# Two-layer hybrid encoder: one split for both key blocks, squares on ScalarE, rotation from SBUF, and head 3's decay moved behind head 0's scores

## The chip, the cores and the metric

The kernel runs on one core of a Trainium2 chip. The metric is the device time of one execution in microseconds (us). The core's engines run beside each other, each with a queue of its own that it works off in order: TensorE (PE in the profile, PEld for its loads of weights) multiplies, VectorE (DVE) and ScalarE (ACT) work elementwise, GpSimd (POOL) does little here, and SyncE (SP) issues the DMAs. Results of TensorE land in PSUM, which is eight banks; operands lie in SBUF.

## The reference

A trunk of two layers. Each has four token mixers beside each other (A to D), merged by gates, and a gated MLP with a convolution. Batch 1, 256 tokens and 16 meta tokens ahead of them; all in float32.

```python
for l in range(DEPTH):                                   # 2 layers, T = 16 + 256 tokens, D_MODEL = 1024
    u = _rms_norm(h, norm_mix_pre[l])
    (a_q, a_k, a_v, b_q, b_k, b_v, b_r, b_g, c_qa, c_kva, c_kr,
     d_q, d_k, d_v, gate_logits) = jnp.split(u @ w_in[l], offsets, axis=-1)
    o_a = _diff_attention(...)   # A: 4 heads, two softmax maps, p0 - lam * p1, RMSNorm over 128 values
    o_b = _gla(...)              # B: 4 heads, both directions, chunks of 64: cumsum of log decay, exp, RMSNorm
    o_c = _mla(...)              # C: 4 heads, queries of 128 + 64 rotated, rank 256 / 128
    o_d = _window_gqa(...)       # D: 8 query heads, 2 key heads, band of 128, sink
    branches = jnp.stack([o_a, o_b, o_c, o_d], axis=2)
    gates = jax.nn.sigmoid(gate_logits.reshape(bsz, T, N_BRANCH, D_MODEL))
    merged = jnp.sum(jnp.einsum('btnw,nwd->btnd', branches, w_branch[l]) * gates, axis=2)
    h = h + _rms_norm(merged @ w_out[l], norm_mix_post[l])
    f = _conv_ffn(_rms_norm(h, norm_ffn_pre[l]), ffn_w_up[l], ffn_conv_w[l], ffn_conv_b[l], ffn_w_down[l])
    h = h + _rms_norm(f, norm_ffn_post[l])
return h[:, N_META:]
```

`_mla` rotates the last 64 of each query head and one key of 64: `x1 * cos - x2 * sin`, `x1 * sin + x2 * cos`. A and B end with an RMSNorm over the 128 values of a head, which needs the sum of squares. In `_gla` the decay of a head is the exponential of a running sum inside chunks of 64.

## The kernel before

Activations are held transposed: features on the 128 partitions, the 272 tokens along the free axis (258 in parts of layer 2). All weights stream once from HBM in blocks of 128x1024 (512 KB): SP's queue loads a block to a `raw` buffer (three of them), ACT casts it to the high half `wh`, and VectorE subtracts that from `raw` to give the low half `wl` (L221, five buffers each). Activations are split in the same way (`split`, L310 to L312: ACT's cast gives the high half, VectorE's subtraction the low half), and each product is three matmuls, high by high, high by low and low by high (`mm3`). A `raw` buffer is reloaded when its `wl` is done. SP's queue holds these loads in order, with the bias loads of A and D (`bA`, `bD`, L283) among them.

Each mixer is a Python generator whose steps are cut by `yield`. `interleave(main, n_main, n_fill, fill)` runs a mixer's steps and puts pieces of other work between them: the next projections, gates and branch products (`pj`, `br` in the profile), some 12 matmuls of 126 ns each at a time. The pairs `N_B1`, `N_B2`, `N_A` and so on are the counts of steps and of fillers for each stage:

```python
interleave(comp_b1(db), *N_B1, fill)      # B: gates, running sums, decay, factors
interleave(comp_b2(db), *N_B2, fill)      # B: keys, states, scores, outputs of each head
...
interleave(comp_a(da), *N_A, fill)        # A, beside gates, B's branch and C's projections
```

A scheduler of the framework then sets each engine's queue from this program order, the data dependencies and its own estimate of durations, so a queue's order is not the program's order, and a change in one place can re-deal the queues of all engines for some distance. An engine that waits holds all that stands behind it in its queue.

PSUM is shared by three pools: `mm` (three banks: projections, `pj`, `qu`, `br`), `sc` (two: scores) and `ax` (three: transposes `tpp`, `tpr`, `tpv`, sums `ps_A`, `ps_B`, outputs `poA`, `poB`, `poC`). A tile of a pool waits until the reader of the tile that had the bank before is done.

The places that the change touches:

- `transpose_p` (A, C, D): for each head, four transposes put the probabilities of two query blocks and two key blocks into one bank (`tpp`), and `split` brings each key block's half to `pth` (ACT) and `ptl` (VectorE); `tpr` holds the 16 remaining keys.
- `square_hl` (A, B): the square of a head's output on VectorE (L520), its cast on ACT (L521), the rest on VectorE (L522); `sum_heads` multiplies both by ones (`ps_A`, `ps_B`), and `aq` (L933) is ACT's copy of `ps_A`.
- `rope` (C): four ACT copies of 32 rows (`sw`, L971) swap the halves, VectorE multiplies them by the sine (L972), the source in PSUM by the cosine with the scale (L976), and adds (L977). The key's rotation has scale 1 and runs in place. `sw` is one tile with one buffer.
- `comp_b1`, the first stage of B: for each head the running sums (L761, L763, both scans), their exponentials, and the products with keys and queries (L769, L770); `factors` after heads 1 and 3; after head 2 also `keys(d, 0)`, after head 3 `states(d, 0)`. `comp_b2` then goes through the heads: keys, states, scores, outputs.

Of the kernel before, what the change touches and what calls it, by code (L numbers as in the profile page):

```python
# [15 lines left out]
AF = mybir.ActivationFunctionType  # L16
# [8 lines left out]
T = 272  # L25
# [13 lines left out]
AHEAD = 2  # L39
GROUP = 4  # L40
N_WARM, N_WARM0 = 12, 16
N_B1, N_B2, N_A, N_CU, N_C, N_D = (8, 24), (15, 17), (24, 30), (7, 12), (20, 24), (35, 36)
LAM_INIT = [0.8 - 0.6 * math.exp(-0.3 * l) for l in range(DEPTH)]

O_AQ, O_AK, O_AV = 0, 512, 1024
# [72 lines left out]
def hybrid_kernel(ctx: ExitStack, tc: tile.TileContext, hT0, w, pc_in, p2_in, cc_in, oh_in, tab_in, gl_in, out):  # L118
# [354 lines left out]
    for l in range(DEPTH):  # L473
# [9 lines left out]
        with ExitStack() as scope:  # L483
# [33 lines left out]
            def square_hl(src):  # L517
                sq, sqh, sql = [tmp.tile([P, T], dt, name="sq", tag=f"sq{i}", bufs=1)[:, cs]
                                for i, dt in enumerate((F32, F32R, F32R))]
                V.tensor_mul(sq, src[:, cs], src[:, cs])  # L520
                S.copy(sqh, sq)  # L521
                V.tensor_sub(sql, sq, sqh.bitcast(F32))  # L522
                return sqh, sql
# [106 lines left out]
            def transpose_p(pts, pair):  # L630
                pth, ptl, ptr = pts
                tp = axb("tpp")
                for qt in range(2):
                    for kc in range(2):
                        PE.transpose(tp[:, kc * 256 + qt * 128:kc * 256 + qt * 128 + 128],
                                     pair[qt][:, kc * 128:kc * 128 + 128], ident)
                for kc in range(2):
                    split(pth[:, kc, 16:T].rearrange("p (a b) -> p a b", a=2),
                          ptl[:, kc, 16:T].rearrange("p (a b) -> p a b", a=2),
                          tp[:, kc * 256:kc * 256 + 256].rearrange("p (a b) -> p a b", a=2)[:, :, ::-1])  # L640
                tr = axb("tpr")
                for qt in range(2):
                    PE.transpose(tr[:16, qt * 128:qt * 128 + 128], pair[qt][:, 256:272], ident)
                put_rem(ptr, 16, 256, tr[:16, :256].rearrange("p (a b) -> p a b", a=2)[:, :, ::-1])
# [81 lines left out]
            def comp_b1(d):  # L726
# [29 lines left out]
                    V.tensor_copy(mq[b, hs, 1:2], two[b, hs, 1:2])  # L756

                G.memset(dec[64:128, :, 0:1], 1.0)
                for h in range(4):
                    b_ = x1[h][0:64, :]  # L760
                    V.tensor_tensor_scan(b_, C("smask", 0, 64), b_, 0.0, ALU.mult, ALU.add)  # L761
                    b_ = x1[h][64:128, ::-1]
                    V.tensor_tensor_scan(b_, C("smask", 64, 128)[:, ::-1], b_, 0.0, ALU.mult, ALU.add)  # L763
                    x3 = cf("x3")
                    act(LN_EXP_SET, x3, x1[h], AF.Exp, scale=-1.0 / 16)
                    act(LN_EXP_SET, x2[h], x1[h], AF.Exp, scale=1.0 / 16)
                    S.copy(dec[0:64, h, :], x2[h][0:64, 15::64])
                    S.copy(dec[64:128, h, 1:5], x2[h][64:128, 16:T:64])
                    V.tensor_mul(ks[h], ks[h], x3)  # L769
                    V.tensor_mul(qs[h], qs[h], x2[h])  # L770
                    if h % 2:
                        factors(slice(h - 1, h + 1))
                    if h == 2:
                        keys(d, 0)
                    if h == 3:
                        states(d, 0)
                    yield

            def by_chunk(t):
                return t.rearrange("p (c t) -> p c t", c=4)  # L780
# [31 lines left out]
            def comp_b2(d):  # L812
# [39 lines left out]
                for h in range(4):  # L852
                    if h:
                        states(d, h)
                        yield
                        norm(h - 1)
                    if h < 3:
                        keys(d, h + 1)
                    scores(h)
                    yield  # L860
                    outputs(h)
                    yield
                yield
# [101 lines left out]
            def rope(dst, src, rows, c0=0, scale=1.0):  # L965

                sw = tmp.tile([P, T], F32, name="sw", tag="sw", bufs=1)
                c = slice(c0, T)
                for b_ in range(0, rows, 32):
                    o = b_ ^ 32  # L970
                    S.activation(sw[b_:b_ + 32, c], src[o:o + 32, c], AF.Copy, scale=scale)  # L971
                V.tensor_mul(sw[:rows, c], sw[:rows, c], C("sin", 0, rows)[:, c])  # L972
                if scale == 1.0:
                    V.tensor_mul(dst[:, c], src[:, c], C("cos", 0, rows)[:, c])
                else:
                    V.scalar_tensor_tensor(dst[:, c], src[:, c], scale, C("cos", 0, rows)[:, c], ALU.mult, ALU.mult)  # L976
                V.tensor_add(dst[:, c], dst[:, c], sw[:rows, c])  # L977

            def proj_c(d, kper):
# [30 lines left out]
            def proj_c_up(d):  # L1010
# [16 lines left out]
                for i in (4, 5, 0, 1, 2, 3):  # L1027
                    ps = mmb("qu")
                    for k in range(2):
                        mm3(ps[:, cs], wq[k][0][:, i * P:(i + 1) * P], wq[k][1][:, i * P:(i + 1) * P], lh[1 + k][:, cs],  # L1030
                            ll[1 + k][:, cs], k == 0, k == 1)
                    qf.append(u(f"cq{i}"))
                    if i >= 4:
                        rope(qf[-1], ps, P, ct, C_SCALE)
                    else:
                        S.activation(qf[-1][:, cs], ps[:, cs], AF.Copy, scale=C_SCALE)
                    if i % 2:
                        yield
                qf[:] = qf[2:] + qf[:2]
# [510 lines left out]
```

## Time and profile before

| | |
|---|---|
| median of 3 runs | 1144.18 us (1143.24 to 1145.17) |
| the profiled execution | 1141.39 us, its span 1139.6 us |
| granted TensorE clock | 0.999 of full speed |
| busy: PE, DVE, ACT | 1115.9 us, 925.2 us, 757.2 us |
| instructions: PE, DVE, ACT | 8678, 2049, 1635 |

The span runs from the first to the last instruction of the core; the time of the execution is 1.8 us longer. The busy time of an engine is the sum of its instructions. A view of waits lists, for each engine, how long it sat idle until another engine (or a DMA) released it, by the names of the two operations. In a timeline each row is an instruction with its start, its duration, and in brackets the idle time just ahead of it and what ended that. Layer 1's mixers run from about 40 to 300 us, layer 2's from about 600 to 900.

### The profile page before, as it was taken

The numbers are of one execution on the slowest core, as the hardware profiler recorded it, in microseconds if no ns is written. First come the engines' busy times: TensorE is split into PE (matmuls) and PEld (weight loads), VectorE is DVE, ScalarE is ACT, GpSimd is POOL, SyncE is SP. The second block draws the span as 40 slices with busy tenths as digits, with TensorE's granted clock in tenths as the row PEclk, the third lists the DMA queues.
The fourth block names the chain that finished last, engine by engine and source line by source line (L and its number), as shares of the span: only waits on it lengthen the run. The fifth ranks groups of instructions, "written<-read, shape, count | busy, mean of one in ns | idle before, by whom it ended". The sixth has DMA issues, their size and how long they took to land.

```text
span 1139.6 us, 22838 instructions
## 1 busy us (share of the span) xinstructions
PE 1115.9 (98%) x8678; PEld 1077.4 (95%) x8678; DVE 925.2 (81%) x2049; ACT 757.2 (66%) x1635; POOL 12.9 (1%) x57
## 2 busy tenths in 40 slices
PE   9999999999999999999999999999999999999997
PEld 8999889999999999999999998999999999999986
DVE  7977986898977799995479868968989769999843
ACT  7855776777765767665458557867787657766632
POOL 1000000000000000000000000000000000000000
PEclk9999999999999999999999999999999999999999
DMA  7642454445646356655546534554356462655552
GB/s 265 219 147 98 130 160 148 139 116 135 179 142 215 109 172 202 183 161 175 181 142 219 148 100 134 144 165 155 115 142 171 164 241 98 204 196 193 185 185 74
DMA packets 60914, 183.73 MB, mean 161 GB/s; under 512 B 10443, under 2 KB 17739, under 8 KB 60420
## 3 DMA queue, kind: packets, MB, share of 16 engines
q1 hardware_dynamic: 60148, 181.36, 51.6%
q8 instruction: 68, 1.11, 0.4%
q10 hardware_dynamic: 656, 0.91, 0.2%
q14 instruction: 42, 0.34, 0.1%
HBM read 180.03 MB, written 2.21 MB: 160 GB/s over the span
## 4 chain that ended last, share of the span: by engine, by line
PE 80%; DVE 8%; ACT 7%; DMA 2%; issue 2%; SPq 0%; DVEq 0%; ACTq 0%
PE pj L183 52%; PE dn L183 6%; PE br L183 6%; PE dt L183 5%; DMA raw<-wst 2%; DVE wl L221 2%; ACT wh L221 2%; PE sc L183 1%; PE poD L183 1%; PE poB L183 1%; PE at L183 1%; PE tpp L186 1%; PE scm L183 1%; ACT p L607 1%; PE kvu L183 1%
## 5 line engine op out<-in xcount | busy, mean ns | idle before, releaser
L183 PE MATMUL pj<-xh,wh 128*128 128x272 f32 (+1 forms) x1888 | 546.6, 292 | 7.3 <-ACT xh L350 3.1
L183 PE MATMUL pj<-xl,wh 128*128 128x272 f32 (+1 forms) x1888 | 540.1, 287 | 0.0
L183 PE MATMUL pj<-xh,wl 128*128 128x272 f32 (+1 forms) x1888 | 540.1, 287 | 0.0
L221 DVE TENSOR_TENSOR wl<-raw,wh 128x1024 fp32r<-128x1024 f32 (+2 forms) x322 | 386.6, 1204 | 105.0 <-ACT wh L221 102.5
L221 ACT CAST wh<-raw 128x1024 fp32r<-128x1024 f32 (+2 forms) x322 | 332.7, 1035 | 192.9 <-PE pj L183 85.1
L183 PEld LDWEIGHTS pj<-xh,wh 128*128 128x128 f32 x1888 | 354.7, 189 | 12.9 <-ACT xh L350 3.7
L183 PEld LDWEIGHTS pj<-xl,wh 128*128 128x128 f32 x1888 | 356.1, 189 | 1.4 <-issue 0.4
L183 PEld LDWEIGHTS pj<-xh,wl 128*128 128x128 f32 x1888 | 355.6, 189 | 0.7 <-issue 0.2
L1357 ACT ACTIVATE cv<-u,pc 128x272 f32<-128x272 f32 (+1 forms) x88 | 52.9, 605 | 12.5 <-DVE u L1355 12.1
L183 PE MATMUL dn<-ah,wh 128*128 128x272 f32 x176 | 51.0, 290 | 0.0
L183 PE MATMUL dn<-al,wh 128*128 128x272 f32 x176 | 50.7, 288 | 0.0
L183 PE MATMUL dn<-ah,wl 128*128 128x272 f32 x176 | 50.5, 287 | 0.0
L1361 DVE SCALAR_TENSOR_TENSOR cv<-u,pc,cv 128x271 f32<-128x271 f32 (+1 forms) x88 | 43.0, 489 | 1.8
L607 ACT ACTIVATE p<-p,st 128x272 f32<-128x272 f32 x68 | 35.1, 516 | 13.8 <-DVE st L605 13.8
L1359 DVE SCALAR_TENSOR_TENSOR cv<-u,pc,cv 128x271 f32<-128x271 f32 (+1 forms) x88 | 42.9, 487 | 1.2 <-ACT cv L1357 0.9
L1202 DVE TENSOR_TENSOR gt<-pj,rs_x 128x272 f32<-128x272 f32 (+1 forms) x64 | 27.4, 429 | 14.3 <-PE pj L183 13.8
L1355 DVE TENSOR_TENSOR u<-pj,rs_x 128x272 f32<-128x272 f32 (+1 forms) x88 | 36.9, 425 | 0.0
L183 PE MATMUL dt<-wh,al 128*128 128x512 f32 x88 | 34.8, 395 | 0.0
L183 PE MATMUL dt<-wh,ah 128*128 128x512 f32 x88 | 34.7, 395 | 0.0
L183 PE MATMUL dt<-wl,ah 128*128 128x512 f32 x88 | 34.5, 392 | 0.0
L183 PEld LDWEIGHTS dn<-al,wh 128*128 128x128 f32 x176 | 33.1, 188 | 0.0
L183 PEld LDWEIGHTS dn<-ah,wh 128*128 128x128 f32 x176 | 33.1, 188 | 0.0
(390 smaller groups left out, 1904.7 us busy)
## 6 DMA issues: line engine op xcount, KB each, us to landing
raw<-wst SPq DMA_DIRECT2D x306, 512.0 KB, 3.7
raw<-wst SPq DMA_DIRECT2D x12, 384.0 KB, 3.2
bD<-bvec SPq DMA_DIRECT2D x16, 256.0 KB, 5.2
bA<-bvec SPq DMA_DIRECT2D x8, 400.0 KB, 5.0
hT<-hT SPq DMA_DIRECT2D x1, 1088.0 KB, 6.6
h_dram<-hT SPq DMA_DIRECT2D x1, 1088.0 KB
hT<-h_dram SPq DMA_DIRECT2D x1, 1088.0 KB, 6.2
raw<-wst SPq DMA_DIRECT2D x4, 256.0 KB, 4.5
```

Source lines behind the costliest of these rows:

```text
L183: self.note(nc.tensor.matmul(*args, **kw))
L186: self.note(nc.tensor.transpose(*args, **kw))
L221: pair = S.copy(wh[:, c], raw[:, c]), V.tensor_sub(wl[:, c], raw[:, c], wh[:, c].bitcast(F32))
L607: S.activation(p, p, AF.Exp, scale=-1.0, bias=st[:, 0:1], accum_out=st[:, 1:2])
L1202: V.tensor_mul(f[:, ct:T], (yield from pj(ct))[:, ct:T], RS[:, ct:T])
L1355: V.tensor_mul(u_[:, ct:T], ps[:, ct:T], RS[:, ct:T])
L1357: S.activation(t[:, cd:T], u_[:, cd:T], AF.Identity, scale=PCc("cw1", c), bias=PCc("cb", c))
L1359: V.scalar_tensor_tensor(t[:, lo:T], u_[:, lo - 1:T - 1], PCc("cw0", c), t[:, lo:T], ALU.mult, ALU.add)
L1361: V.scalar_tensor_tensor(t[:, cd:T - 1], u_[:, cd + 1:T], PCc("cw2", c), t[:, cd:T - 1], ALU.mult, ALU.add)
```

## The change

It has four parts. `transpose_p` splits both key blocks in one operation for each engine (512 columns in place of twice 256). `square_hl` takes the square on ACT. `rope` for the queries first copies the PSUM bank to SBUF with the scale on ACT, and VectorE multiplies that copy by the cosine; the bank then has readers on ACT only. In B, the decay of head 3 and the factors of heads 2 and 3 move from the first stage into the second, behind the scores of head 0; `keys(d, 0)` and `states(d, 0)` become steps of their own, and each of the two stages counts one step more, with as many fillers as before.

```diff
@@ -39,7 +39,7 @@
 AHEAD = 2
 GROUP = 4
 N_WARM, N_WARM0 = 12, 16
-N_B1, N_B2, N_A, N_CU, N_C, N_D = (8, 24), (15, 17), (24, 30), (7, 12), (20, 24), (35, 36)
+N_B1, N_B2, N_A, N_CU, N_C, N_D = (9, 24), (16, 17), (24, 30), (7, 12), (20, 24), (35, 36)
 LAM_INIT = [0.8 - 0.6 * math.exp(-0.3 * l) for l in range(DEPTH)]
 
 O_AQ, O_AK, O_AV = 0, 512, 1024
@@ -517,7 +517,7 @@
             def square_hl(src):
                 sq, sqh, sql = [tmp.tile([P, T], dt, name="sq", tag=f"sq{i}", bufs=1)[:, cs]
                                 for i, dt in enumerate((F32, F32R, F32R))]
-                V.tensor_mul(sq, src[:, cs], src[:, cs])
+                S.activation(sq, src[:, cs], AF.Square)
                 S.copy(sqh, sq)
                 V.tensor_sub(sql, sq, sqh.bitcast(F32))
                 return sqh, sql
@@ -634,10 +634,9 @@
                     for kc in range(2):
                         PE.transpose(tp[:, kc * 256 + qt * 128:kc * 256 + qt * 128 + 128],
                                      pair[qt][:, kc * 128:kc * 128 + 128], ident)
-                for kc in range(2):
-                    split(pth[:, kc, 16:T].rearrange("p (a b) -> p a b", a=2),
-                          ptl[:, kc, 16:T].rearrange("p (a b) -> p a b", a=2),
-                          tp[:, kc * 256:kc * 256 + 256].rearrange("p (a b) -> p a b", a=2)[:, :, ::-1])
+                split(pth[:, :, 16:T].rearrange("p k (a b) -> p k a b", a=2),
+                      ptl[:, :, 16:T].rearrange("p k (a b) -> p k a b", a=2),
+                      tp.rearrange("p (k a b) -> p k a b", k=2, a=2)[:, :, :, ::-1])
                 tr = axb("tpr")
                 for qt in range(2):
                     PE.transpose(tr[:16, qt * 128:qt * 128 + 128], pair[qt][:, 256:272], ident)
@@ -756,7 +755,9 @@
                     V.tensor_copy(mq[b, hs, 1:2], two[b, hs, 1:2])
 
                 G.memset(dec[64:128, :, 0:1], 1.0)
-                for h in range(4):
+
+                def decay(h):
+
                     b_ = x1[h][0:64, :]
                     V.tensor_tensor_scan(b_, C("smask", 0, 64), b_, 0.0, ALU.mult, ALU.add)
                     b_ = x1[h][64:128, ::-1]
@@ -768,13 +769,21 @@
                     S.copy(dec[64:128, h, 1:5], x2[h][64:128, 16:T:64])
                     V.tensor_mul(ks[h], ks[h], x3)
                     V.tensor_mul(qs[h], qs[h], x2[h])
-                    if h % 2:
-                        factors(slice(h - 1, h + 1))
-                    if h == 2:
-                        keys(d, 0)
-                    if h == 3:
-                        states(d, 0)
+
+                def late():
+                    decay(3)
+                    factors(slice(2, 4))
+
+                d["late"] = late
+                for h in range(3):
+                    decay(h)
+                    if h == 1:
+                        factors(slice(0, 2))
                     yield
+                keys(d, 0)
+                yield
+                states(d, 0)
+                yield
 
             def by_chunk(t):
                 return t.rearrange("p (c t) -> p c t", c=4)
@@ -858,6 +867,9 @@
                         keys(d, h + 1)
                     scores(h)
                     yield
+                    if not h:
+                        d["late"]()
+                        yield
                     outputs(h)
                     yield
                 yield
@@ -970,10 +982,7 @@
                     o = b_ ^ 32
                     S.activation(sw[b_:b_ + 32, c], src[o:o + 32, c], AF.Copy, scale=scale)
                 V.tensor_mul(sw[:rows, c], sw[:rows, c], C("sin", 0, rows)[:, c])
-                if scale == 1.0:
-                    V.tensor_mul(dst[:, c], src[:, c], C("cos", 0, rows)[:, c])
-                else:
-                    V.scalar_tensor_tensor(dst[:, c], src[:, c], scale, C("cos", 0, rows)[:, c], ALU.mult, ALU.mult)
+                V.tensor_mul(dst[:, c], dst[:, c], C("cos", 0, rows)[:, c])
                 V.tensor_add(dst[:, c], dst[:, c], sw[:rows, c])
 
             def proj_c(d, kper):
@@ -1030,10 +1039,9 @@
                         mm3(ps[:, cs], wq[k][0][:, i * P:(i + 1) * P], wq[k][1][:, i * P:(i + 1) * P], lh[1 + k][:, cs],
                             ll[1 + k][:, cs], k == 0, k == 1)
                     qf.append(u(f"cq{i}"))
+                    S.activation(qf[-1][:, cs], ps[:, cs], AF.Copy, scale=C_SCALE)
                     if i >= 4:
                         rope(qf[-1], ps, P, ct, C_SCALE)
-                    else:
-                        S.activation(qf[-1][:, cs], ps[:, cs], AF.Copy, scale=C_SCALE)
                     if i % 2:
                         yield
                 qf[:] = qf[2:] + qf[:2]
```

How it moves the queues, at four places. In the rows, the number with L is the line, then the operation, out<-in by the names of the program, the tile's size, and with x how many follow each other.

ACT in layer 1, at the rotation of the queries (`qu` is the bank of the up-projected queries, `gt` a gate, `cq` a query chunk). Before:

```order
L221 CAST wh<-raw 128x1024 x2
L163 ACTIVATE gt_2702<-gt_2702 128x272
L971 ACTIVATE sw<-qu 32x272 x8
L163 ACTIVATE gt_2792<-gt_2792 128x272
L221 CAST wh<-raw 128x1024
L1036 ACTIVATE cq_2833<-qu 128x272
L1036 ACTIVATE cq_2842<-qu 128x272
L311 CAST qmAh<-cq_2833 128x16
```

After:

```order
L221 CAST wh<-raw 128x1024 x2
L163 ACTIVATE gt_2694<-gt_2694 128x272
L1042 ACTIVATE cq_2759<-qu 128x272
L983 ACTIVATE sw<-qu 32x272 x4
L1042 ACTIVATE cq_2776<-qu 128x272
L983 ACTIVATE sw<-qu 32x272 x4
L163 ACTIVATE gt_2786<-gt_2786 128x272
L1042 ACTIVATE cq_2827<-qu 128x272
L221 CAST wh<-raw 128x1024
```

Each rotation now begins with a copy of its bank, and the eight swap copies are parted by the second one's copy.

ACT in layer 2, in attention A, from the exponentials of head 1's first query block (`p` and its sums `st`) to the copy of the sums of squares of head 0 (`aq`); `av` is a head's output. Before:

```order
L607 ACTIVATE p,st<-p,st 128x272 x2
L948 COPY av_8938<-poA 128x258
L626 CAST ptr_117<-tmA 16x16
L627 CAST ptr_117<-tmA 16x16
L521 CAST sq<-sq 128x258
L163 ACTIVATE gt_9448<-gt_9448 128x258
L221 CAST wh<-raw 128x1024
L607 ACTIVATE p,st<-p,st 128x272 x2
L163 ACTIVATE gt_9524<-gt_9524 128x258
L933 COPY aq_8455<-ps_A 128x258
```

After:

```order
L607 ACTIVATE p,st<-p,st 128x272 x2
L960 COPY av_8919<-poA 128x258
L626 CAST ptr_117<-tmA 16x16
L520 ACTIVATE sq<-av_8919 128x258
L627 CAST ptr_117<-tmA 16x16
L521 CAST sq<-sq 128x258
L221 CAST wh<-raw 128x1024
L163 ACTIVATE gt_9416<-gt_9416 128x258
L607 ACTIVATE p,st<-p,st 128x272 x2
L221 CAST wh<-raw 128x1024
L945 COPY aq_8434<-ps_A 128x258
```

The squares stand on ACT; one weight cast now stands ahead of the gate, and a second one between the exponentials and `aq`. In layer 1 the same place has the two casts in the same order, where before a gate and the exponentials preceded the only cast ahead of `aq`.

ACT in layer 1, in attention C at head 2 (`dkh` is the split of D's keys, `vrA` and `ptr` the 16 remaining keys, `scC` scores). Before:

```order
L311 CAST pth<-tpp 128x256
L626 CAST ptr_115<-tpr 16x256
L627 CAST ptr_115<-tpr 16x256
L311 CAST pth<-tmC 128x2x16
L532 CAST vrA<-tpv 16x128
L533 CAST vrA<-tpv 16x128
L221 CAST wh<-raw 128x1024
L311 CAST pth<-tpp 128x256
L603 ACTIVATE p,st<-scC,st 128x272
```

After:

```order
L311 CAST vh<-tpv 128x256
L311 CAST pth<-tpp 128x2x256
L311 CAST dkh_3236<-pf 64x272
L1120 CAST dkh_3236<-pf 64x272
L626 CAST ptr_115<-tpr 16x256
L627 CAST ptr_115<-tpr 16x256
L311 CAST pth<-tmC 128x2x16
L532 CAST vrA<-tpv 16x128
L533 CAST vrA<-tpv 16x128
L221 CAST wh<-raw 128x1024
```

The second half of the transposed probabilities had stood behind a weight cast; both halves now stand ahead of it.

VectorE in layer 2, attention A, up to the low half `ql` of a head's queries. Before, from the second `p` of the scores on:

```order
L605 ISA p,st<-sc,bA 128x272
L605 ISA st 128x1
L221 TENSOR_TENSOR wl<-raw,wh 128x1024
L611 RECIPROCAL st<-st 128x1 x2
L520 TENSOR_TENSOR sq<-av_8938 128x258
L926 TENSOR_TENSOR st<-st,neglam 128x1
L927 TENSOR_SCALAR p<-p,st 128x272
L1202 TENSOR_TENSOR gt_9448<-pj,rs_x 128x258
L928 SCALAR_TENSOR_TENSOR p<-p,st 128x272
L522 TENSOR_TENSOR sq<-sq 128x258
L312 TENSOR_TENSOR ql<-aq_8539,qh 128x256
```

After, the stretch with `ql` stands earlier than those scores:

```order
L312 TENSOR_TENSOR vl<-tpv,vh 128x256
L611 RECIPROCAL st<-st 128x1
L312 TENSOR_TENSOR ql<-aq_8509,qh 128x256
L938 TENSOR_TENSOR st<-st,neglam 128x1
L312 TENSOR_TENSOR ptl<-tpp,pth 128x2x256
L940 SCALAR_TENSOR_TENSOR p<-p,st 128x272
L534 TENSOR_TENSOR vrA<-tpv,vrA 16x128
L628 TENSOR_TENSOR ptr_117<-tpr,ptr_117 16x256
L312 TENSOR_TENSOR ptl<-tmA,pth 128x2x16
L628 TENSOR_TENSOR ptr_117<-tmA,ptr_117 16x16
L1210 TENSOR_TENSOR gt_9323<-pj,rs_x 128x258
L605 ISA p,st<-sc,bA 128x272
```

`ql` moved from behind a whole step of softmax to just behind `vl`.

In SP's queue the loads of the weights keep their order among themselves; relative to the bias loads they stand one or two places earlier at bias loads of A (the third and fourth of each layer) and D.

## The prediction

> **What bounds the kernel now.** I read the page first (shares), then the waits of TensorE, then the timeline round each wait that the change can touch.
>
> ```profile
> span 1139.6 us, 22838 instructions
> ...
> PE 1115.9 (98%) x8678; PEld 1077.4 (95%) x8678; DVE 925.2 (81%) x2049; ACT 757.2 (66%) x1635; POOL 12.9 (1%) x57
> ```
>
> TensorE (PE) is busy for 1115.9 of 1139.6 us; neither VectorE (DVE) nor ScalarE (ACT) is near that. Less work on DVE is therefore worth nothing in itself: it pays only where a matmul stands waiting for it. The change leaves TensorE's matmuls as they are, so its whole effect is in TensorE's waits. Those that lie in the mixers:
>
> ```profile
> PE pj L183 <- DVE cq L976: 1.9, 2, 1.0
> ...
> PE poC L183 <- DVE vrA L534: 1.4, 2, 0.8
> PE sc L183 <- DVE ql L312: 1.3, 2, 0.8
> PE pj L183 <- DVE r L540: 1.2, 1, 1.2
> PE tpr L186 <- ACT aq L933: 1.2, 1, 1.2
> ...
> PE tpv L186 <- DVE vpl L312: 0.7, 2, 0.4
> PE poC L183 <- ACT pth L311: 0.5, 1, 0.5
> PE ps_A L183 <- ACT sq L521: 0.4, 2, 0.2
> ```
>
> The columns are the total in us, the number of waits and the longest. These eight sum to 8.6 us, which is about all there is to win, 0.75% of the span; the other rows of that view stand at the norms between sub-layers and at the start, which the change does not touch.
>
> **The change part by part.** Times of places are us from the start of the span; layer 1 is the half up to about 560, layer 2 the rest.
>
> *Work per engine.* The durations:
>
> ```profile
> L312 DVE TENSOR_TENSOR ptl<-tpp,pth x64: 400/418/426, 121.7 to 893.7; 128x256 fp32r<-128x256 f32 x64
> L311 ACT CAST pth<-tpp x64: 351/372/383, 121.3 to 893.2; 128x256 fp32r<-128x256 f32 x64
> L520 DVE TENSOR_TENSOR sq<-av x8: 419/430/443, 127.0 to 733.6; 128x272 f32<-128x272 f32 x4, 128x258 f32<-128x258 f32 x4
> L514 ACT ACTIVATE sq<-cl x6: 411/427/432, 168.6 to 746.9; 128x272 f32<-128x272 f32 x4, 128x258 f32<-128x258 f32 x2
> ```
>
> Sixteen squares (eight in A, eight in B) leave DVE, at most 16 x 0.43 = 6.9 us, and arrive on ACT as 16 of the kind of the last row, again at most 6.9 us. The 64 splits of 256 columns become 32 of 512 on both engines. I take away one fixed part of a tenth of a microsecond per pair (an estimate: in the timeline below four 32-row copies take 1.59 us in a row, and the steps inside overlap by about that), some 3 us on each engine. The four rotations keep their multiply on DVE (now from SBUF) and add four copies of at most 0.43 us on ACT. So DVE loses 10 us of 925 and ACT gains about 5 of 757. None of it is on TensorE's path except at the places that follow; everywhere else it is hidden by TensorE's own 98%, and I cost it at nothing.
>
> *Rotation of the queries (C, step of the up-projection).*
>
> ```profile
> 198.18 1.59 ACT L971 ACTIVATE sw<-qu 32x272 f32<-32x272 f32 x4 [1.42 <-DVE cq L977]
> 199.81 0.44 DVE L972 TENSOR_TENSOR sw<-sw,cc 128x272 f32<-128x272 f32 x1 [0.98 <-ACT sw L971]
> 200.16 0.43 DVE L976 SCALAR_TENSOR_TENSOR cq<-qu,cc 128x272 f32<-128x272 f32 x1
> 200.74 0.36 PE L183 MATMUL pj<-xh,wh 128*128 128x272 f32 x1 [0.85 <-DVE cq L976]
> ```
>
> The second rotation's PSUM bank is read by four ACT copies (198.18 to 199.77) and then by DVE until 200.59; the gate's product, which takes that bank next, starts at 200.74. ACT had been idle for 1.42 us before the copies, waiting for DVE to let go of the one scratch tile `sw`. In the change both readers of the bank are on ACT, and the copy `cq` of the second rotation falls into that idle time. The bank is then free at the end of the swap copies. These start somewhat later, because the first rotation's own copy stands ahead of its swaps on ACT (+0.3: the copy `aq` in the rows below takes 0.38 and overlaps with the next): 198.45 + 1.6 = 200.05 instead of 200.59. Gain 0.5 in layer 1, and as much in layer 2, where the order is the same: **-1.0** of the row's 1.9. Bounds: -1.9 if the first rotation's copy is hidden too, +0.6 if both copies simply lengthen ACT's chain. The Trainium skill, "PSUM — Partial Sum Buffer", section "PSUM bank collisions raise a hardware error", says that two engines must not access one bank at once and that the scheduler puts a dependency between them. The rows agree (DVE reads `qu` only after ACT has ended); were the two reads allowed side by side, the bank would already be free at 199.8 and this term would be a small loss, and the sum -1.3 instead of -2.6.
>
> *One split for both key blocks (C).*
>
> ```profile
> 237.84 1.05 ACT L221 CAST wh<-raw 128x1024 fp32r<-128x1024 f32 x1
> 238.79 0.37 ACT L311 CAST pth<-tpp 128x256 fp32r<-128x256 f32 x1
> 239.21 0.39 PE L183 MATMUL poC<-pth,vh 128*128 128x272 f32 x1 [0.48 <-ACT pth L311]
> 239.67 0.39 PE L183 MATMUL poC<-ptl,vh 128*128 128x272 f32 x1
> ...
> 256.61 0.29 PE L183 MATMUL poC<-ptl,vh 128*128 128x272 f32 x1
> 256.74 0.29 PE L183 MATMUL poC<-pth,vl 128*128 128x272 f32 x1
> ```
>
> The second half's cast stood behind a weight cast of 1.05 us; the output product waited 0.48 for it, then some 0.3 more for `ptl` (it starts 0.46 after its neighbour, where 0.13 is the step of two that do not wait, as at 256.61 and 256.74). In the change both halves are cast ahead of that weight cast: gain 0.8 to 0.9. At the next head (256) only the second `ptl` goes, 0.45, the start itself waits for `vrA` as before; in layer 2 likewise about 0.25. Against that `vpl`, the value split of the first head of D, is queued behind the longer `ptl` on DVE and comes some 0.3 later in each layer, and its wait (0.7 in two) grows by about that less TensorE's own gain: +0.35. Together **-1.2**; ends -1.6 (no loss at D) and 0. A and D showed no wait of TensorE for a second half.
>
> *Decay of head 3 after the scores of head 0 (B).* In the first stage DVE is the full engine:
>
> ```profile
> 620.00:630.00 10.00, 8.81 (x74) 8.60 (x73) 9.84 (x27) 7.06 (x19) 0.00 (x0) 1.00 0.49 147
> ```
>
> (the window's length, then PE, PEld, DVE, ACT, POOL, clock, DMA share, GB/s). The one wait there (1.2, for the bank that the `r` product left to DVE) is set by what stands ahead of the copy on DVE. In both orders most of head 3's decay already lay behind that copy; what goes is two products of the factors and one query product, what comes is one multiply by the query and one by the cosine. That makes the copy 0.3 earlier: **-0.3**, ends -1.2 and +0.5. The moved part is done between the scores and outputs of head 0, where no row shows TensorE waiting for DVE and where the squares leave DVE free: nothing, ends 0 and +1.
>
> *Attention A.* Here the queue of each engine changes most, and two effects oppose each other. Layer 2:
>
> ```profile
> 705.35 1.05 ACT L221 CAST wh<-raw 128x1024 fp32r<-128x1024 f32 x1 [2.03 <-DMA raw<-wst]
> 706.31 0.52 ACT L607 ACTIVATE p<-p,st 128x272 f32<-128x272 f32 x1
> 707.64 0.35 ACT L933 COPY aq<-ps_A 128x258 f32<-128x258 f32 x1
> 704.01 0.39 PE L183 MATMUL sc<-akh,ql 64*128 64x272 f32 x2 [0.81 <-DVE ql L312]
> 706.57 0.60 PE L186 MATMUL tpp<-cc,p 128*128 128x128 f32 x4
> 708.05 0.39 PE L186 MATMUL tpr<-cc,p 128*16 128x128 f32 x2
> ```
>
> For the better: `ql` moves ahead on DVE to just behind `vl`, far before the scores that need it, so the waits of the row on `ql` (1.3 in all, 0.81 here) go. For the worse: `tpr` needs the bank that the copy `aq` empties. That copy stood behind one weight cast, which itself waited 2.03 us for its DMA; in the change two weight casts stand ahead of it. The second adds one step of 0.95 (706.31 less 705.35 is 0.96), less some 0.4 (an estimate) because the first cast's load is now issued ahead of a bias load and not behind it: `aq` at about 708.2, so `tpr` at 708.6 instead of 708.05. In the change TensorE has only 4 filling matmuls between `tpp` and `tpr` and not 8, so four steps of 0.12 are still to come: 708.6 + 0.5 - 708.05, about +1.0 here with the gain at `ql` already in it. Layer 1:
>
> ```profile
> 125.42 1.22 DVE L221 TENSOR_TENSOR wl<-raw,wh 128x1024 fp32r<-128x1024 f32 x1
> 131.43 1.05 ACT L221 CAST wh<-raw 128x1024 fp32r<-128x1024 f32 x1 [0.66 <-DMA raw<-wst]
> 132.39 0.38 ACT L933 COPY aq<-ps_A 128x272 f32<-128x272 f32 x1
> 132.82 0.39 PE L186 MATMUL tpr<-cc,p 128*16 128x128 f32 x2
> ...
> 143.70 1.05 ACT L221 CAST wh<-raw 128x1024 fp32r<-128x1024 f32 x1 [0.99 <-DMA raw<-wst]
> 144.99 0.37 ACT L933 COPY aq<-ps_A 128x272 f32<-128x272 f32 x1
> ```
>
> The first cast now precedes a gate and two softmax exponentials, and a second cast follows these: 130.3 (its load, 3.7 us after DVE's half of the block that held its buffer, the row at 125.42, has ended, which the change moves little) + 0.95 + 0.33 + 0.95 + 0.95 + 0.33 gives `aq` at about 133.9 and `tpr` at 134.2, 1.4 later than before with 5 of the filling matmuls (0.63) already done: +0.75, again with the 0.6 of `ql` in it. The wait of 1.2 at the next head (`aq` at 144.99, behind a cast that waited 0.99 for its load) goes, since VectorE's halves of the weights, which release the raw buffers, now come earlier: -1.3 with the restart. The small waits at `ps_A`, and at the later `tpr` of layer 2, whose chain loses a change of engine and a 0.43 operation: -0.5. Sum for A: +1.0 + 0.75 - 1.3 - 0.5 = **-0.1**; ends -3.4 (no new wait) and +3 (the same wait at one more head of each layer).
>
> *Sum:* -1.0 - 1.2 - 0.3 - 0.1 = -2.6 us. The profiled execution would go from 1141.39 to 1138.8. That execution stands 2.8 us below the median of the runs (1144.18); the same difference taken off the median gives **1141.6 us**. A change of less than 0.2%, 2.3 us, can hardly be told from none here.
>
> **The rivals.**
>
> 1. *Waits are only exchanged.* The new wait at `tpr` comes at full size in both layers, the rotation gains nothing because ACT's chain is as much longer as DVE's is shorter, and only the split in C pays: between -1 and +1.5, near 1143.8. For it: ACT's casts are tied to loads of 3.7 us, and eight places are re-dealt with only one in view of TensorE.
>
> ```profile
> raw<-wst SPq DMA_DIRECT2D x306, 512.0 KB, 3.7
> ```
>
> Against it: the 0.85 at 200.74 and 0.48 at 239.21 have a plain cause that is gone.
>
> 2. *Slower: weight casts that wait for their load hold up ACT in A.* Each cast that now stands ahead of the exponentials and of `aq` blocks all behind it. Price 1.7 to 2.2 us a time at `tpr` (layer 2 without the credit for `ql`). It happens once in each layer in my sum; if it happens at a second head of each, A is +3, and the total +0.5 to +1.5; with a third, or with the exponentials late enough to delay `tpp`, +4: about 1148. It decides from three such heads on. Against it: after one such wait TensorE is late and the loads have caught up, and the transposes of a head use exponentials one step older (`tpp` at 706.57 stands only 0.26 behind the start of a pair of exponentials that it cannot be using), so these have some 3 us in hand. The Trainium skill, "PSUM — Partial Sum Buffer", section "Engine vs sequencer instructions", calls ScalarE's queue strictly first in, first out. The rows at 705.35 and 706.31 agree: 2.03 us idle with an exponential ready behind.
>
> 3. *All of it goes.* The earlier halves on DVE bring the loads forward far enough that no cast waits, and the eight rows shrink to 2 or 3 us: -6, about 1138, at most -8.6, 1135.6.
>
> 4. *The squares make ACT the late engine.* It is at 66% and in B's windows below 75%; I give it no more than a part of rival 1.
>
> **How the numbers follow.** My forecast, between -2.3 and -4, has 0.38; with rival 3 (0.15) that makes faster 0.50, the rest of the forecast's spread (0.03) falling within 0.2%. Within: rival 1, 0.32, and that 0.03: 0.35. Slower: rival 2, 0.15. The range from 1137.5 (rival 3 in most of its extent) to 1146.0 (rival 2 up to two heads, and the spread of runs, 1143.24 to 1145.17) leaves out the far ends of 2 and 3.
>
> **What would show it.** Right: the row for `cq` among TensorE's waits gone or near 0.9 and a wait on ACT's `sw` or `cq` in its place; no wait on the second `pth`; no wait on `ql`; a wait of 1 to 2 us at `tpr` for `aq` at about 133 and 707 and none at 145; DVE near 915 us, ACT near 762. Wrong: a row of more than 2 us for `aq`, `p` or `pth` on ACT, a new wait of the scores of B's heads for DVE, or a wait for weights (`wh` or `wl`) in the mixers.

## The result, and the profile after

The changed kernel takes 1137.71 us (1137.49 to 1138.01, 4 runs) against 1143.97 us (1143.24 to 1145.17): a ratio of 0.9947, 95% interval 0.9935 to 0.9959, or 6.3 us less. The two profiled executions, 1141.39 and 1137.86 us, are only 3.5 us apart. Both differences have to be explained.

The page of the changed kernel, its span and the shares:

```profile
span 1136.1 us, 22808 instructions
...
PE 1113.3 (98%) x8678; PEld 1077.5 (95%) x8678; DVE 918.8 (81%) x2001; ACT 760.9 (67%) x1623; POOL 12.8 (1%) x57
```

VectorE lost 6.4 us and ScalarE gained 3.7; TensorE's matmuls are the same. The waits of TensorE in the mixers (total, times, longest):

```profile
PE tpv L186 <- DVE vpl L312: 1.5, 4, 0.5
...
PE tpr L186 <- ACT aq L945: 1.4, 3, 0.8
PE pj L183 <- DVE gt L1210: 1.3, 2, 0.7
...
PE tpv L186 <- DVE bvf L540: 0.7, 1, 0.7
PE ps_A L183 <- ACT sq L521: 0.6, 2, 0.4
PE poC L183 <- DVE ptl L312: 0.6, 2, 0.3
PE pj L183 <- DVE r L540: 0.5, 1, 0.5
...
PE poC L183 <- DVE ptr L628: 0.3, 2, 0.2
...
PE pj L183 <- ACT sw L983: 0.3, 1, 0.3
```

Gone are the rows for `cq` (1.9), `vrA` (1.4), `ql` (1.3) and `pth` (0.5). New are `gt` (1.3), `bvf` (0.7) and smaller ones, and `vpl` has doubled. The eight rows of the prediction come to 4.0 us in place of 8.6.

To see where the time went I compare the start of the same matmul, counted from the first, in both traces, at eleven places of the program. The numbers are how much more (+) or less (-) each stretch takes than in the profiled execution of before, in us. Where a kernel's matmuls stand in another order, a boundary can be off by some 0.2. "ctrl" and the others are the experiments below.

| kernel | to 38 us | B, layer 1 | A | up-projection of C | C | D and MLP | B, layer 2 | A | up-projection | C | rest | sum |
|---|---|---|---|---|---|---|---|---|---|---|---|---|
| changed | +0.4 | 0.0 | -1.8 | 0.0 | -1.0 | 0.0 | +0.3 | -1.2 | 0.0 | -1.0 | +0.4 | -3.9 |
| ctrl | -0.9 | +0.5 | +0.3 | 0.0 | 0.0 | 0.0 | -0.1 | +0.9 | 0.0 | 0.0 | +0.5 | +1.2 |
| split | -0.6 | +0.7 | -1.7 | 0.0 | -1.0 | 0.0 | -0.1 | +2.3 | +0.2 | -0.8 | +0.4 | -0.5 |
| square | 0.0 | +1.3 | -0.5 | +0.1 | 0.0 | 0.0 | 0.0 | +3.2 | 0.0 | -0.1 | +0.7 | +4.7 |
| rope | -0.6 | +0.4 | +2.2 | +0.1 | 0.0 | +0.1 | 0.0 | +1.0 | +0.4 | +0.4 | +0.5 | +4.5 |
| late | +0.9 | -0.3 | -1.3 | 0.0 | 0.0 | 0.0 | +0.1 | -1.1 | 0.0 | 0.0 | +0.5 | -1.2 |
| no_rope | +0.5 | -0.1 | -1.8 | -0.1 | -1.0 | 0.0 | 0.0 | -1.4 | 0.0 | -0.8 | +0.4 | -4.2 |
| no_late | +0.2 | +1.0 | -1.0 | +0.1 | -1.0 | 0.0 | +0.8 | -1.2 | +0.7 | -1.0 | +0.5 | -0.8 |
| no_square | -0.4 | -0.8 | -1.1 | +0.1 | -1.0 | 0.0 | 0.0 | -0.4 | +0.5 | -1.0 | +0.5 | -3.7 |
| late_split | -0.5 | -0.4 | -1.1 | +0.1 | -1.0 | 0.0 | 0.0 | -0.9 | +0.1 | -0.9 | +0.5 | -4.1 |
| raw4 | -0.6 | -1.2 | -1.9 | +0.3 | -1.2 | 0.0 | -0.7 | -1.4 | +0.6 | -0.9 | +0.5 | -6.6 |

The changed kernel wins 3.0 in A and 2.0 in C, and nothing at the rotation or in B. `ctrl`, the unchanged kernel once more, differs from before by up to 0.9 in a single stretch; only A and C stand clear of that. The sum ends at the last matmul. What follows it takes 0.4 us longer in the changed kernel, so the executions are 3.5 us apart and not 3.9.

### The profile page after: what moved, and what is told of

Read it like the earlier page. It is cut to its first block, busy times and chain, and to the rows that moved or that the text cites. A ratio compares the mean times of both kernels' runs of the same rounds, so it can differ in the third digit from the quotient of the medians.

```text
span 1136.1 us, 22808 instructions
## 1 busy us (share of the span) xinstructions
PE 1113.3 (98%) x8678; PEld 1077.5 (95%) x8678; DVE 918.8 (81%) x2001; ACT 760.9 (67%) x1623; POOL 12.8 (1%) x57
## 4 chain that ended last, share of the span: by engine, by line
PE 77%; DVE 9%; ACT 8%; DMA 3%; issue 2%; DVEq 0%; SPq 0%; ACTq 0%
PE pj L183 49%; PE br L183 7%; PE dn L183 6%; PE dt L183 5%; DMA raw<-wst 3%; DVE wl L221 2%; ACT wh L221 2%; PE poD L183 1%; PE sc L183 1%; PE poB L183 1%; PE at L183 1%; PE tpp L186 1%; ACT p L607 1%; ACT sw L983 1%; PE kvu L183 1%
```

## The experiments

All times are medians beside runs of the kernel before on the same chip (medians 1143.39, 1143.00 and 1143.25 there), and the ratio is to those.

| kernel | what | median us | ratio, 95% interval |
|---|---|---|---|
| split | one split alone | 1141.36 | 0.9981 (0.9972 to 0.9990) |
| square | squares alone | 1145.55 | 1.0021 (1.0011 to 1.0030) |
| rope | rotation alone | 1145.57 | 1.0017 (1.0008 to 1.0025) |
| late | late decay alone | 1139.41 | 0.9965 (0.9951 to 0.9978) |
| late_split | these two | 1138.70 | 0.9957 (0.9945 to 0.9970) |
| no_rope | all but the rotation | 1136.91 | 0.9944 (0.9931 to 0.9956) |
| no_square | all but the squares | 1138.03 | 0.9954 (0.9940 to 0.9967) |
| no_late | all but the late decay | 1139.40 | 0.9968 (0.9956 to 0.9981) |
| before_raw5 | before, 5 raw buffers, 4 pairs | 1142.78 | 0.9998 (0.9990 to 1.0007) |
| after_raw5 | changed, 5 raw buffers, 4 pairs | 1136.14 | 0.9936 (0.9923 to 0.9950) |
| raw4 | changed, 4 raw buffers, 5 pairs | 1135.29 | 0.9931 (0.9918 to 0.9943) |

**Each part alone.** The edits are the hunks of the change: of `transpose_p` (split), of `square_hl` (square), of `rope` and its call (rope), and of `comp_b1`, `comp_b2` and the counts (late).

> Only the split of both key blocks in one operation, the rest as before. Theory A (the gain is the sum of waits that each part ends where it stands): the waits of the output products in C go, those of vpl at D grow a little: -1 to -1.5 us against the kernel before, and nothing in B or at the rotation. Theory B (the gain comes of how the queues are re-dealt as a whole): anything from -4 to +2 us, with waits of TensorE changed at places that this part does not touch.

> Only the squares of A and B on ScalarE, the rest as before. Theory A: the waits at ps_A and part of those at ql and aq in A go: -0.5 to -1.5 us. Theory B: up to -4 us (with 7 us less on VectorE the halves of the weights come earlier everywhere), or +2.

> Only the rotation of the queries from SBUF, the rest as before. Theory A: the waits for the bank of the second rotation shrink from 1.9 to about 1: -1 us, and nothing elsewhere. Theory B: -3 to +2 us with other places changed.

> Only head 3's decay and the later factors behind head 0's scores, with one step more in each stage of B, the rest as before. Theory A: the wait for the bank of r in layer 2 shrinks by 0.3 to 0.7 and a wait of the same size appears at the transposes of B's values: 0 us within 0.5. Theory B: -3 to +2 us with other places changed.

Measured, each ratio applied to 1143.4 us: -2.2, +2.4, +1.9 and -4.0 us. They sum to -1.9 where all four together give -6.3: the parts do not add up, and two of them alone cost about 2 us where a gain of 0.5 to 1.5 was expected. Theory A holds for the places of the split (-1.0 and -0.8 in the two C stretches) and falls for the other three.

First `rope`. Up to the rotation its queues on ScalarE and VectorE are those of the kernel before, and still attention A in layer 1 took 2.2 us more. Its timelines there, ScalarE's cast and TensorE's rows around the wait:

```profile
144.65 1.04 ACT L221 CAST wh<-raw 128x1024 fp32r<-128x1024 f32 x1 [2.23 <-DMA raw<-wst]
...
146.35 0.39 PE L186 MATMUL tpr<-cc,p 128*16 128x128 f32 x2 [2.42 <-ACT aq L933]
...
147.88 0.43 PE L183 MATMUL pj<-xl,wh 128*128 128x272 f32 x1
148.11 0.43 PE L183 MATMUL pj<-xh,wl 128*128 128x272 f32 x1
```

This is the wait of 1.2 us that the prediction showed for `aq` (its row at 144.99) in the kernel before, in an execution in which the load landed later: SP's queue issued it at 137.92 us, 0.3 earlier than in the trace of before (138.21), and the cast that waits for it started at 144.65 and not 143.70. The cost does not end with the wait. At 147.9 the matmuls take 0.43 us and follow each other by 0.23, not 0.126. The windows (length, PE, PEld, DVE, ACT, POOL busy, then the granted clock) of `rope` first and of the kernel before second:

```profile
147.70:151.00 3.30, 3.30 (x18) 2.80 (x17) 2.71 (x11) 3.25 (x7) 0.00 (x0) 0.51 0.02 6
```

```profile
147.70:151.00 3.30, 3.30 (x29) 3.19 (x26) 3.26 (x11) 3.27 (x6) 0.00 (x0) 1.00 0.21 49
```

The granted clock is 0.51 for 3.3 us, and 18 rows of matmuls stand where 29 did: an estimate from these figures is that a wait of 2.4 us costs 1 to 1.4 us more after it has ended (1.4 for 11 matmuls of 0.126; 1.0 is what is left of the 2.2 when the longer wait is taken off). The same happens in `square` and `split`, in layer 2's A, where their columns are +3.2 and +2.3. Their rows for `aq`, and their windows behind the longest of these waits, `square` first:

```profile
PE tpr L186 <- ACT aq L933: 4.5, 3, 2.8
...
724.00:726.00 2.00, 2.00 (x11) 1.52 (x10) 1.58 (x5) 1.44 (x3) 0.00 (x0) 0.50 0.53 152
```

```profile
PE tpr L186 <- ACT aq L932: 2.4, 1, 2.4
...
730.00:732.00 2.00, 2.00 (x11) 2.00 (x11) 1.75 (x5) 1.32 (x4) 0.00 (x0) 0.50 0.05 8
```

How much of this is the parts' own doing? In `rope` the queues of ScalarE and VectorE in A are those of the kernel before in both layers. The long wait is therefore not the rotation's; it is one that the unchanged kernel's queues allow too. At its own places and behind them `rope` takes 0.1 us more in layer 1's up-projection and 0.4 each in layer 2's up-projection and C. These 0.9 us are the low end of what its interval gives (0.9 to 2.9); where the rest of the median's 1.9 comes from stays open. In `square` the queues in A are dealt anew, and A takes 2.7 us more (`ctrl` 1.2). Elsewhere the squares cost little: B of layer 2 shows 0.0, and of the +1.3 in B of layer 1 some 1.0 arises between 38 and 48 us, ahead of the first square (73 us), where `ctrl` takes 0.6 more too. So in the profiled execution the squares alone are slower mainly through A's wait for a load; one trace does not show that for the median.

Then `late`. It gains 4.0 us, but not where its work was moved. The waits of ScalarE's weight casts for a load, in the kernel before, from 113 to 165 us and from 688 to 745 us (A in layers 1 and 2):

```profile
ACT wh L221 <- DMA raw<-wst: 2.4, 3, 1.0
...
ACT wh L221 <- DMA raw<-wst: 2.8, 3, 2.0
```

In these stretches the changed kernel, `late_split`, `no_rope` and `no_square` have no such row at all, and `late` has 1.1 us. The kernels without the late decay have 5.1 (`ctrl`), 7.2 (`rope`), 4.3 (`split`), 3.8 (`square`) and 2.9 us (`no_late`). What differs is when VectorE works off the low halves that release the raw buffers. In the changed kernel the half that releases the buffer for the load ahead of layer 1's first `aq`, the 33rd block of weights counted from the first, and that load:

```profile
115.78 1.22 DVE L221 TENSOR_TENSOR wl<-raw,wh 128x1024 fp32r<-128x1024 f32 x1
...
117.06 0.33 SPq L204 DMA_DIRECT2D raw<-wst  x1
```

In the kernel before they stand at 125.42 and 126.71. This half ends between 115 and 118 us in the five kernels with the late decay and three raw buffers, and between 122 and 128 in the six without it. Whether the moved work does it, or the added step in each stage of B, which spreads the fillers anew, no run separates.

**The kernel before once more.** The unchanged kernel, profiled on another chip.

> The kernel before, unchanged, profiled once more. Theory C (the kernel before varies from run to run with the landing of weight loads in front of ScalarE's casts in attention A): an execution near its median of 1143.4 us has 2 to 3 us more wait of tpr for aq (rows of PE on ACT aq) than the profiled execution of 1141.39 us, and nothing else of more than 0.5 us differs. Rival: the difference is spread over all 322 casts, no single wait over 0.5 us.

It took 1142.56 us, 1.2 more than the profiled execution of before. The two A stretches have 0.3 and 0.9 more (row "ctrl" of the table); the start, B of layer 1 and the end (-0.9, +0.5, +0.5) cancel. Its row for `aq` is 1.6 in two waits, not 1.2 in one:

```profile
PE tpr L186 <- ACT aq L933: 1.6, 2, 1.3
```

The expectation named 2 to 3 us more of wait, for an execution near the median of 1143.4; this one is faster than that, and 0.4 came, with the rest in smaller waits. The place is right and the size is not. `rope`, with the same queues in A, shows that the long wait with the lower clock behind it can come; that the runs of before up to 1145.45 us have it is argued and not shown, since none of them was profiled.

**More raw buffers.** The edit is one line.

```diff
-NRAW, NWH = 3, 5
+NRAW, NWH = 5, 4
```

> The kernel before with five raw buffers and four pairs of split weights in place of three and five (the same memory): loads are issued two blocks earlier, so that no cast should wait for one. Theory C: the waits of tpr for aq go and with them the spread of the runs (now 1141.15 to 1145.45): -2 to -4 us, spread below 1.5 us. Rival (the waits at tpr come of the order of the queues, not of loads): no change, 0 within 1 us; or slower because a pair of split weights comes free later.

> The changed kernel with five raw buffers and four pairs of split weights. Theory C: little is left for it to win, since its casts wait for loads less often: 0 to -1.5 us against the changed kernel (1137.7), 1136.2 to 1137.7. Rival: slower, 1139 or more, where the fourth pair of split weights comes free too late.

ScalarE's waits for loads, and TensorE's waits at the norms, of before first and of `before_raw5` second:

```profile
ACT wh L221 <- DMA raw<-wst: 23.8, 26, 2.6
...
PE ps_post L183 <- ACT sqn L331: 1.4, 3, 0.5
```

```profile
ACT wh L221 <- DMA raw<-wst: 1.2, 2, 0.6
...
PE ps_post L183 <- ACT sqn L331: 3.9, 3, 1.3
```

The loads are hardly waited for any more and no row for `aq` is left; the spread of the runs fell to 1.8 us (1141.95 to 1143.73) from 2.9 beside it, though not below the 1.5 expected. The waits behave as theory C has it. The time does not: -2 to -4 us was expected, and the ratio is 0.9998. The norms wait 2.5 us longer, which goes with four pairs of split weights (with five, in `raw4` below, they are at 1.4), and A, with the queues dealt anew, takes 0.6 us more in layer 1 and 0.3 less in layer 2 than in the trace of before. On the changed kernel the same edit gave 1136.14, at the edge of what was expected; its interval overlaps that of the changed kernel.

**Two parts together, and three of four.**

> Two of the four parts: the late decay and the one split; squares on VectorE and rotation from PSUM as before. If the parts add up (late -4.0, split -2.0, square +2.2, rope +2.2 alone): -6.0, 1137.4, as fast as all four. If late and split win by the same waits in A: -4.5, 1139. If the squares and the rotation only cost time in themselves, it beats all four: 1135 or less.

> The changed kernel with the rotation as before. ScalarE's queue in A is row for row that of the changed kernel. Theory D (the rotation is worth nothing: its bank wait is exchanged for one of the next gate, and the gain sits in A and C): 1137.7 within 0.5 us. Rival (the rotation alone cost 2.2 us, and costs that here too): 1135.5. Rival (it gains the 1.0 us that its own wait shows): 1138.7.

> The changed kernel with the squares on VectorE. A's order on ScalarE is nearly that of late and split together (1138.7). Theory D: 1138 to 1139. Rival (the squares alone cost 2.2 us, and cost that here too): 1135.5.

> The changed kernel with B's stages as before. Theory D: A is dealt in another order (aq with no or one weight cast close ahead), so A's gain of 3 us is open, from none to all of it; C's 2.0 us stay. With a wait at tpr above 2.3 us in either layer and the lower clock behind it: 1141 to 1144; without: 1138 or less. Rival (the late decay is what gains, -4.0 alone): 1141.7.

`late_split` came out at 1138.70, as "the same waits in A" has it, and with the 0.8 to 1.0 in each C that the split shows everywhere. `no_rope`, whose queue on ScalarE in A is the changed kernel's, has its ratio (0.9944 against 0.9947), though its median lies 0.8 us below the 1137.7 that was expected within 0.5: no gain and no cost of the rotation is seen in this company. The intervals alone would leave room for 1 to 2 us either way; the traces (-4.2 and -3.9) differ by 0.3. `no_square` is 0.0007 above the changed kernel, 0.8 us, and the intervals overlap; a gain of the squares in this company is possible and its size open, a cost of 2.2 is excluded. `no_late` loses 2.4 us of the 6.3 (the intervals just touch), the largest of the three parts that were left out; by the table some 1.5 of the difference lies in B and 0.8 in A. Its longest wait at `tpr` is 1.2, for which theory D had 1138 or less: 1139.40 is a miss. More is left than the rival would have (1141.7): A is dealt in a third way and still wins 1.0 and 1.2 us. All four without the split was not run; its worth rests on the C stretches, which take 0.8 to 1.2 us less in every kernel of the table that has it and in no other.

**A fourth raw buffer.** The changed kernel with a fourth raw buffer, and two of the mixers' tiles given up for the room:

```diff
-NRAW, NWH = 3, 5
+NRAW, NWH = 4, 5
...
-NS, NX, NB = 19, 8, 12
+NS, NX, NB = 17, 8, 12
```

> The changed kernel with four raw buffers and five pairs of split weights, the room taken from two of the 19 tiles for mixer values. With the loads a block earlier and the split weights as many as before: the casts' waits for loads fall (21 us in the changed kernel), tpr's waits for aq (1.4) go, the waits at the norms stay at 1.4 and not 3.9: 1134 to 1136, faster than with five and four (1136.1). Rival: two tiles fewer make VectorE or ScalarE wait for a free tile in the mixers: 1138 or more.

1135.29 us (1134.69 to 1136.58), 8.0 below the kernel before. Its ratio is 0.0016 (1.8 us) below that of the changed kernel, and the intervals overlap: that it is faster than the changed kernel is likely and not shown. The waits that it was made for, and its new one:

```profile
ACT wh L221 <- DMA raw<-wst: 7.2, 10, 1.5
...
PE qu L183 <- DVE gt L1210: 2.7, 2, 1.4
...
PE ps_post L183 <- ACT sqn L331: 1.4, 3, 0.5
...
PE tpr L186 <- ACT aq L945: 1.1, 3, 0.5
```

The loads cost ScalarE a third of what they cost in the changed kernel (21.0), the norms stay at 1.4, `aq` falls only to 1.1 where it should have gone, and a wait of the up-projection for a gate (2.7) takes back about 1 us (+0.3 and +0.6 in the table). The gain over the changed kernel sits in B (2.2 in both layers) and in the first stretch, not in A.

## Why the prediction was right or wrong

The time lies at the low end of the range, and the sign was right; the forecast of -2.6 us was 40% of the 6.3 measured. That the time still lies in the range is partly luck: the terms came out otherwise, and 2.8 us of the gain lie in the distance between the profiled execution and the median, which the sum took as fixed. What came is near rival 3 (-6), which had a chance of 0.15. Its mechanism came true in A, where no cast waits for a load any more; over the whole span the casts still wait 21.0 us (23.8 before), and the eight rows came to 4.0, not 2 or 3. By the prediction's own terms, against the -3.9 of the two traces (the first and the last stretch have the remaining +0.8):

- *Rotation, -1.0 forecast, 0.0 measured in both layers.* The mechanism of the first step was right: the wait for the bank fell to 0 and 0.3, better than forecast. The step that failed is what is late next. The gate's product that follows waits for the next bank, which VectorE empties only behind the query splits:

```profile
204.02 0.39 PE L183 MATMUL pj<-xh,wh 128*128 128x272 f32 x1 [0.61 <-DVE gt L1210]
...
768.18 0.39 PE L183 MATMUL pj<-xh,wh 128*128 128x258 f32 x1 [0.30 <-ACT sw L983]
773.48 0.39 PE L183 MATMUL pj<-xh,wh 128*128 128x258 f32 x1 [0.71 <-DVE gt L1210]
```

  The prediction followed one bank and not the one after it. Rival 1 had this outcome, for another reason (a longer chain on ScalarE).
- *One split, -1.2 forecast, -2.0 measured.* Right in mechanism and mis-sized: layer 2 gave as much as layer 1 (1.0), where 0.25 had been put down, and the loss at `vpl` is real (0.8 more in its row) and contained in these numbers.

```profile
236.90 0.36 PE L183 MATMUL poC<-pth,vh 128*128 128x272 f32 x1 [0.32 <-DVE ptl L312]
...
244.69 0.28 PE L186 MATMUL tpv<-cc,pf 128*16 128x128 f32 x1 [0.43 <-DVE vpl L312]
```

- *Late decay in B, -0.3 forecast, +0.3 measured.* The wait for the bank of `r` fell by 0.7 (1.2 to 0.5), more than forecast, and the same 0.7 appeared ahead of it, in front of the transposes that wait for the copy of B's values (`bvf`). Alone, this part gains in A (-1.3 and -1.1), which the next term bears on:

```profile
616.13 0.50 PE L186 MATMUL tpv<-cc,bvf 128*16 128x128 f32 x3 [0.70 <-DVE bvf L540]
619.98 0.39 PE L183 MATMUL pj<-xh,wh 128*128 128x258 f32 x1 [0.50 <-DVE r L540]
```

- *A, -0.1 forecast, -3.0 measured.* This is the term that was most mis-sized. The waits on `ql` and the wait of 1.17 at the later `aq` went as forecast, and the new waits at `tpr` came where they were put; but the new ones are 0.43 and 0.76, not about 1.3 and 1.8:

```profile
128.59 1.04 ACT L221 CAST wh<-raw 128x1024 fp32r<-128x1024 f32 x1
130.52 0.43 ACT L163 ACTIVATE gt<-gt 128x272 f32<-128x272 f32 x1 [0.88 <-DVE gt L1210]
...
133.18 0.36 ACT L945 COPY aq<-ps_A 128x272 f32<-128x272 f32 x1
133.60 0.39 PE L186 MATMUL tpr<-cc,p 128*16 128x128 f32 x2 [0.43 <-ACT aq L945]
...
700.08 1.05 ACT L221 CAST wh<-raw 128x1024 fp32r<-128x1024 f32 x1
704.52 0.37 ACT L945 COPY aq<-ps_A 128x258 f32<-128x258 f32 x1
704.94 0.39 PE L186 MATMUL tpr<-cc,p 128*16 128x128 f32 x2 [0.76 <-ACT aq L945]
```

  The step that failed is the landing of the first cast's load: put at 130.3 and, in layer 2, at about 704.9, while the casts started at 128.59 and 700.08 without any wait. It rested on the premise that the change moves VectorE's half at 125.42 little. The same half now starts at 115.78, and the one that counts in layer 2 at 686.11 in place of 699.97, so the loads are issued some 10 and 14 us earlier. That goes with the late decay, whose price the prediction had sought in B alone; without it A still wins 2.2 (`no_late`), with 2.9 us of waits for loads. What ScalarE then waited for was VectorE's gate (0.88). The second cast did stand ahead of `aq`, as forecast.
- *Work per engine.* VectorE's work fell by 6.4 us and ScalarE's rose by 3.7, where 10 and 5 had been estimated. Neither engine bounds the kernel, as the prediction had it.
- *From the execution to the median.* The prediction carried the 2.8 us between them over to the changed kernel. That was wrong: the changed kernel's runs lie within 0.5 us of its profile, while those of before spread over 4 us above theirs. The profiled execution of before was near the fastest that it had (1141.15 to 1145.45 in 51 further runs). The part of the gain that the two traces do not show, 2.8 us, is this spread: the changed kernel is steadier. `ctrl` has 1.2 us more in A than the trace of before, 0.4 of it in waits for `aq`, and `rope`, with the same queues there, 3.2, most of it behind one weight load; A's casts no longer wait for loads in the changed kernel. That the slower runs of before lose their time there is argued from this and not shown.

Rival 2, slower through casts in A, is what the profiled execution of `square` shows: three waits for `aq`, one of 2.8 us, in a kernel that is 2.4 us slower. It was the right mechanism at a price that was too low, since the clock behind the wait was left out. One reading beside it was wrong: no exponential stood ready during the 2.03 us ahead of 705.35, since VectorE wrote its input only from 705.00 on. `rope` shows what was meant: the gate at 145.60 had its input at 142.44 and stood behind the cast that waited for its load until 144.65.

## What to carry to other kernels

Before a gain is read from one trace, look at the spread of the runs: a trace near the fastest run hides the waits that the others have, and a wait for a load on an in-order queue is the first candidate. A part that is slower alone need not be slower in company where a scheduler deals the queues anew; compare stretch by stretch, at the same matmul, before blaming the instructions that were added, and compare the queues there too: a wait in a stretch whose queues did not change is not the part's doing. Work that is moved can pay far from its place, here by letting the operations that release load buffers come earlier. When a wait for a PSUM bank is removed, follow the next bank too.

## What the runs showed of the hardware

A single wait of TensorE of 2.4 to 2.8 us was followed, in three traces (`rope`, `square`, `split`), by 3.41 us at a granted clock of 0.50; waits of 1.2 to 1.4 us (`tpr` in the kernel before and `ctrl`, `qu` in `raw4`) were not. The Trainium skill, "TensorE: Matmul & The Clock Gate", section "Why this matters for your kernels", advises against idle gaps of more than about 3 us; here a gap of 2.4 us was enough, and the measurement decides.

The low clock begins 0.7 to 1.4 us after the wait has ended, because the clock is not granted anew at any moment: in each trace the changes of the granted clock lie whole multiples of 3.41 us apart (42 of them from 4.38 to 147.74 us in `rope`). The stretch of that length ahead of the drop in `rope`, and the slow one:

```profile
144.33:147.74 3.41, 1.39 (x12) 1.38 (x13) 1.52 (x4) 3.06 (x9) 0.00 (x0) 1.00 0.46 171
147.74:151.15 3.41, 3.41 (x17) 2.91 (x17) 2.82 (x11) 3.35 (x7) 0.00 (x0) 0.50 0.02 6
```

TensorE was busy for 1.39 us of such a stretch in `rope`, 1.03 in `split` and 0.67 in `square`. Stretches with 1.57 us (at the end of `no_square`) and with 2.04 us (at the first norm wait of `before_raw5`) were not followed by a drop. These figures fit a clock that goes by how little TensorE worked within one such stretch; three drops are too few to tell that from the length of a single wait.
